# PEER experts of a decoder block: 32 of 256 tokens by fetched expert rows, 224 tokens dense, all up steps ahead of one down pass

## The chip, the cores and the metric

The kernel runs on one core of a Trainium2 chip. The metric is the device time of one execution in microseconds (us). Before the change it is 2338.79 us, the median of three executions (2336.44 to 2342.29). The engines that matter are TensorE (PE; PEld is its weight load, a row of its own), VectorE (DVE), ScalarE (ACT), GpSimd (POOL) and SyncE (SP), the last of which here only issues DMAs. Every engine takes its own instructions in a fixed order.

## The reference, cut to what matters

The block first mixes 256 tokens of width 2048 (sparse attention, a pooling branch, an output projection). The change leaves that part as it is. Then comes PEER: each token picks 8 x 16 = 128 of 16384 single-neuron experts by a product of two key lists, and sums what they give.

```python
def peer_channel_mixer(h, w_peer_q, peer_keys, peer_u, peer_v):
    ...                                   # sub: scores against 2 x 128 keys, 8 heads
    s_top, i_top = lax.top_k(sub, PEER_TOPK)                       # 16 of 128, twice
    cand = s_top[..., 0, :, None] + s_top[..., 1, None, :]
    cand_idx = i_top[..., 0, :, None] * PEER_KEYS + i_top[..., 1, None, :]
    ...
    best, pos = lax.top_k(cand, PEER_TOPK)                         # 16 of 256
    experts = jnp.take_along_axis(cand_idx, pos, axis=-1)
    gates = jax.nn.softmax(best, axis=-1)
    ...
        u = peer_u[ec]
        a = jax.nn.gelu(jnp.einsum('cd,ced->ce', hc, u), approximate=False)
        vv = peer_v[ec]
        return jnp.einsum('ce,ced->cd', (a * gc), vv)
```

`peer_u` and `peer_v` are 16384 rows of 2048 float32 each, 128 MB a table.

## The kernel before

All tokens go through all experts densely. A gate matrix, 16384 experts by 256 tokens and zero where a token did not pick the expert, keeps what counts. The experts come in 128 blocks of 128, the blocks in 4 chunks of `CH` = 32, and the stages follow each other in the order up 0, up 1, down 0, down 1, up 2, up 3, down 2, down 3.

To keep float32 accuracy each product is made of three matmuls (`mm3`, L129 to L133): a float32 operand is split into a rounded high part and the rest (`split`, L117 to L123). ACT casts the high part `wH` (L121), DVE subtracts it from the source to give `wL` (L122). There are three buffers each of `wH` and `wL`, half a block apiece, so the splitters can run one and a half blocks ahead of PE. Weights land in `raw`, four buffers of 1 MB (`RAW`), by DMAs that SP issues (L110 to L115).

`up` (L738 to L745) holds a block of `u` as weights, 128 x 128 at a time, and streams the 256 tokens past: 16 x 3 matmuls of 256 columns a block, then a Gelu on ACT (L744) into `r1` to `r4`. `down` (L762 to L797) holds activations as weights (`aH` L776, `aL` L777) and streams rows of `v` past, 512 columns a matmul: 24 matmuls for each block and half of the output, 48 in all.

Beside `up` runs side work in pieces: the routing (top 16 lists L581 to L584, decoding, softmax), 32 calls of `gates_build` (L697 to L725) that make the gate matrix from one-hot tiles on DVE (L707 to L710), PE (L718) and ACT (L721) and write it to device memory by 16 POOL DMAs, the last 16 rows of the modulation matrix (`ada`, L135 to L138, one DVE pass of 128 x 2048 each), and turning `x` token-first (L752). `step` hands out 1.25 pieces a block (`R_G`) and a modulation row every fourth block (`R_U`). `gates_apply` (L727 to L733) reads the gates back and multiplies. The source order is not the last word: the framework's scheduler interleaves the pieces and fixes the order on each engine when the program is built.

Of the kernel before, what the change touches and what calls it, by code (L numbers as in the profile page):

```python
# [39 lines left out]
def kernel(  # L40
# [647 lines left out]

    def new_a(c):
        if c % 2 == 0:  # L690
            return [px.tile([P, ND, T], F32, name=f"r{i}") for i in (2, 3)]
        return [main.tile([P, ND, T], F32, name="r1"), px.tile([P, ND, T], F32, name="r4")]

    gdram = dram.tile([P, 64, P, 4], F32, name="gdram")
    gstage = {}

    def gates_build(x):  # L697
        t1 = TB * x
        o2 = px.tile([P, TB // 2, P, 2], F16, name="o2", bufs=2)
        o1 = [px.tile([P, TB // 2, P, 2], F16, name=f"o1{q}", bufs=1 + q) for q in range(2)]  # L700

        def per_token(src):
            return (src[:, t1:t1 + TB].rearrange("p (g t) -> p g t", t=2)[:, :, None, :]
                    .to_broadcast([P, TB // 2, P, 2]))

        every = iota2[:, None].to_broadcast([P, TB // 2, P, 2])
        dve.tensor_tensor(o2, every, per_token(idxT[1]), ALU.is_equal)  # L707
        dve.tensor_tensor(o1[1], every, per_token(idxT[0]), ALU.is_equal)
        for q in range(2):
            dve.tensor_tensor(o1[q], o1[1], per_token(gT[q]), ALU.mult)  # L710
        if x % 2 == 0:
            gstage[0] = stream.tile([P, D], F32, name="raw", bufs=RAW)
        for y in range(2):
            ps = gps.tile([P, 512], F32, name="gp")
            for i in range(4):
                for q in range(2):
                    g, k = 2 * y + i // 2, i % 2
                    pe.matmul(ps[:, P * i:P * i + P], o2[:, g, :, k], o1[q][:, g, :, k],  # L718
                              start=q == 0, stop=q == 1)
            n = 2 * (x % 2) + y  # L720
            act.mul(gstage[0][:, 512 * n:512 * n + 512].rearrange("p (i t) -> p i t", t=4),  # L721
                    ps.rearrange("p (t i) -> p i t", i=P), 1.0 / GATE_SCALE)
        if x % 2 == 1:
            g = 2 * (x - 1)
            nc.gpsimd.dma_start(out=gdram[:, g:g + 4].rearrange("p g i t -> p (g i t)"), in_=gstage[0])  # L725

    def gates_apply(a, c, z):  # L727
        raw = stream.tile([P, D], F32, name="raw", bufs=RAW)
        raw = raw.rearrange("p (g i t) -> p g i t", g=16, t=4)
        nc.sync.dma_start(out=raw, in_=gdram[:, 16 * z:16 * z + 16, CH * c:CH * c + CH])  # L730
        for k in range(2):
            av = a[k][:, :, 64 * z:64 * z + 64].rearrange("p i (g t) -> p i g t", t=4)
            dve.tensor_tensor(av, av, raw[:, :, 16 * k:16 * k + 16].rearrange("p g i t -> p i g t"), ALU.mult)  # L733

    def g_pieces(a, c):
        return [lambda z=z: gates_apply(a, c, z) for z in range(4)]

    def up(c, a, per_unit):  # L738
        for e in range(CH):
            ps = accp.tile([P, 512], F32, name="acc")[:, :T]  # L740
            w = load_split(u_in[CH * c + e])
            for d in range(ND):
                mm3(ps, w[d // 8], (d % 8) * P, hH[:, d], hL[:, d], d == 0, d == ND - 1)
            act.activation(a[e // 16][:, e % 16], ps, AF.Gelu)  # L744
            per_unit(e)  # L745

    xtok = xT.rearrange("p j (t d) -> p j t d", t=2)

    def flip_x(q, t):
        ps = gps.tile([P, 512], F32, name="gp")  # L750
        for i in range(4):
            pe.transpose(ps[:, P * i:P * i + P], xtok[:, 4 * q + i, t], ident)  # L752
        act.copy(xtok[:, 4 * q:4 * q + 4, t], ps.rearrange("p (i d) -> p i d", d=P))
# [176 lines left out]
```

## Time and profile before

| what | value |
|---|---|
| median of three executions | 2338.79 us (2336.44 to 2342.29) |
| profiled execution, its own time | 2337.39 us |
| its span, first to last instruction | 2335.5 us |
| PE busy | 2248.0 us, 96% |
| DVE busy | 1577.1 us, 68% |
| ACT busy | 1043.2 us, 45% |
| mean of the DMAs | 226 GB/s |
| mean granted TensorE clock | 0.981 of full speed |

The profiled execution's own time is 1.9 us above its span. A stretch of the span is read by what each engine did in it: an engine that is busy all the time bounds the stretch, and an engine that idles there costs nothing. The time of one matmul is read from the starts of neighbouring ones, since matmuls overlap in the pipeline and each is longer than the distance to the next.

### The profile page before, as it was taken

How to read it: one execution, taken by the hardware profiler on the slowest of the kernel's cores; microseconds unless marked ns; L12 is line 12 of the kernel's file. 1: busy time of each engine (PE TensorE's matmuls, PEld its weight loads, DVE VectorE, ACT ScalarE, POOL GpSimd, SP SyncE). 2: the span in 40 equal slices, each digit the busy share in tenths (PEclk: the TensorE clock that was granted, in tenths of full speed). 3: DMA queues.
4: the chain of work that ended last, by engine and by line, in shares of the span. 5: the costliest groups of instructions: out<-in, count | busy, mean ns of one | idle time of the engine just before them, and what ended most of it. 6: DMA issues, size and time to landing. Idle time of an engine off the chain costs nothing.

```text
span 2335.5 us, 37425 instructions
## 1 busy us (share of the span) xinstructions
PE 2248.0 (96%) x15280; PEld 2061.2 (88%) x15280; DVE 1577.1 (68%) x2419; ACT 1043.2 (45%) x1555; POOL 12.9 (1%) x27
## 2 busy tenths in 40 slices
PE   6999999999989988998899999999999999999998
PEld 5899987999989988997898888889999999888887
DVE  7888877779687998586556656655445445566565
ACT  4543441844344443344444444444444444444443
POOL 0000000000000000000000000000000000000000
PEclk7999999999999999998999999999999999999999
DMA  8888865688755644655587555455457556655563
GB/s 332 334 316 305 299 239 216 247 296 311 283 219 214 227 167 181 245 210 209 219 268 243 184 192 194 184 191 188 181 181 246 192 186 210 232 192 185 189 208 109
DMA packets 126414, 527.02 MB, mean 226 GB/s; under 512 B 8425, under 2 KB 46337, under 8 KB 85793
## 3 DMA queue, kind: packets, MB, share of 16 engines
q1 hardware_dynamic: 123794, 507.68, 60.2%
q0 software_dynamic: 2448, 16.94, 1.8%
q8 instruction: 120, 1.97, 0.3%
q14 instruction: 52, 0.43, 0.0%
HBM read 505.71 MB, written 18.89 MB: 225 GB/s over the span
## 4 chain that ended last, share of the span: by engine, by line
PE 85%; DVE 9%; DMA 4%; issue 1%; ACT 1%; DVEq 0%; ACTq 0%
PE acc L133 16%; PE acc L131 16%; PE acc L132 16%; PE acc L784 10%; PE acc L783 10%; PE acc L785 10%; DMA raw<-in_ada_dram 2%; PE acc L504 2%; DVE wL L122 2%; DVE raw L137 2%; PE gp L718 1%; DVE o L710 1%; DMA raw<-in_wgrp_dram 1%; ACT wH L121 1%; PE mps L206 0%
## 5 line engine op out<-in xcount | busy, mean ns | idle before, releaser
L122 DVE TENSOR_TENSOR wL<-raw,wH 128x1024 fp32r<-128x1024 f32 (+2 forms) x738 | 873.1, 1187 | 589.6 <-ACT wH L121 588.6
L121 ACT CAST wH<-raw 128x1024 fp32r<-128x1024 f32 (+2 forms) x738 | 751.8, 1021 | 1020.5 <-PE acc L132 580.6
L131 PE MATMUL acc<-hH,wH 128*128 128x256 f32 x3248 | 931.1, 287 | 19.1 <-ACT wH L121 17.6
L133 PE MATMUL acc<-hH,wL 128*128 128x256 f32 x3248 | 926.5, 286 | 9.2 <-DVE wL L122 8.8
L132 PE MATMUL acc<-hL,wH 128*128 128x256 f32 x3248 | 925.8, 285 | 0.1
L131 PEld LDWEIGHTS acc<-hH,wH 128*128 128x128 f32 x3248 | 630.3, 194 | 23.9 <-ACT wH L121 21.1
L133 PEld LDWEIGHTS acc<-hH,wL 128*128 128x128 f32 x3248 | 628.9, 194 | 13.8 <-DVE wL L122 13.5
L132 PEld LDWEIGHTS acc<-hL,wH 128*128 128x128 f32 x3248 | 630.4, 194 | 0.8 <-DVE hL L568 0.3
L784 PE MATMUL acc<-wH,aL 128*128 128x512 f32 x1024 | 404.7, 395 | 0.2
L785 PE MATMUL acc<-wL,aH 128*128 128x512 f32 x1024 | 404.1, 395 | 0.0
L783 PE MATMUL acc<-wH,aH 128*128 128x512 f32 x1024 | 400.3, 395 | 0.0
L137 DVE CUSTOM_DVE_ANT_0 raw<-raw,cb 128x2048 f32<-128x2048 f32 x96 | 219.5, 2286 | 32.9 <-DMA raw<-in_ada_dram 32.6
L784 PEld LDWEIGHTS acc<-wH,aL 128*128 128x128 f32 x1024 | 193.0, 188 | 47.4 <-DVE aL L777 2.8
L783 PEld LDWEIGHTS acc<-wH,aH 128*128 128x128 f32 x1024 | 192.9, 188 | 45.0
L785 PEld LDWEIGHTS acc<-wL,aH 128*128 128x128 f32 x1024 | 192.9, 188 | 44.8
L777 DVE TENSOR_TENSOR aL<-r,aH 128x256 fp32r<-128x256 f32 x256 | 106.5, 417 | 0.0
L776 ACT CAST aH<-r 128x256 fp32r<-128x256 f32 x256 | 102.1, 400 | 6.5 <-PE acc L785 3.3
L744 ACT ACTIVATE r<-acc 128x256 f32<-128x256 f32 x128 | 48.6, 380 | 75.0 <-PE acc L133 75.0
L710 DVE TENSOR_TENSOR o<-o,gT 128x1024 f16<-128x1024 f16 x64 | 43.9, 686 | 49.2 <-PE gp L718 49.2
L718 PE MATMUL gp<-o,o 128*128 128x128 f16 x512 | 44.8, 237 | 32.1 <-DVE o L710 26.4
L132 PE MATMUL acc<-m,wH 128*128 128x256 f32 x256 | 72.1, 282 | 0.0
L718 PEld LDWEIGHTS <-o 128*128 128x128 f16 x512 | 34.3, 106 | 38.1 <-DVE o L710 20.0
(216 smaller groups left out, 1447.3 us busy)
## 6 DMA issues: line engine op xcount, KB each, us to landing
raw<-in_u_dram SPq DMA_DIRECT2D x128, 1024.0 KB, 4.8
raw<-in_v_dram SPq DMA_DIRECT2D x128, 1024.0 KB, 4.9
raw<-in_ada_dram SPq DMA_DIRECT2D x96, 1024.0 KB, 5.9
raw<-in_wgrp_dram SPq DMA_DIRECT2D x43, 768.0 KB, 6.3
raw<-in_ybr_dram SPq DMA_DIRECT2D x16, 1024.0 KB, 6.8
raw<-in_wga_dram SPq DMA_DIRECT2D x16, 1024.0 KB, 4.9
raw<-in_wout_dram SPq DMA_DIRECT2D x16, 1024.0 KB, 5.7
raw<-in_wpq_dram SPq DMA_DIRECT2D x16, 1024.0 KB, 5.9
```

The lines of the kernel that those rows point to most:

```text
L121: act.copy(wH[:, :n], src)
L122: dve.tensor_tensor(wL[:, :n], src, wH[:, :n], ALU.subtract)
L131: pe.matmul(ps, wH, xH, start=start, stop=False, **kw)
L132: pe.matmul(ps, wH, xL, start=False, stop=False, **kw)
L133: pe.matmul(ps, wL, xH, start=False, stop=stop, **kw)
L137: dve.tensor_tensor_reduce(raw, raw, cb, scale=1.0, scalar=0.0, op0=ALU.mult, op1=ALU.add, accum_out=modr[:, i:i + 1])
L718: pe.matmul(ps[:, P * i:P * i + P], o2[:, g, :, k], o1[q][:, g, :, k], start=q == 0, stop=q == 1)
L776: act.copy(aH, src)
L777: dve.tensor_tensor(aL, src, aH, ALU.subtract)
L783: pe.matmul(ps[t][k], tH, wH[:, vs], start=first, stop=False)
L784: pe.matmul(ps[t][k], tL, wH[:, vs], start=False, stop=False)
L785: pe.matmul(ps[t][k], tH, wL[:, vs], start=False, stop=final)
```

## The change

The first 32 tokens (`AS`) leave the dense path. For them the code fetches the expert rows by index: four copies of 32 tokens lie on 128 partitions (`SG` = 4), each partition has 32 of the 128 experts of its token, and 32 gathers of 128 rows of `u` and 32 of `v` (8 KB a row, 1 MB a gather, issued by POOL at L787) bring them into two buffers that share the old tile `r1`. DVE makes each dot product with the token (`sparse_up`, one 128 x 2048 pass a gather, L799) and each weighted sum (`sparse_down`, L813 and L815). Each DVE pass, once issued in the code, is followed by the fetch two further on, which takes the buffer that the pass frees. `tokens_h` lays the tokens out for it.

The other 224 tokens (`N`) stay dense. `up` runs over all 128 blocks at a stretch and stores its activations to device memory (`adram`) by an ACT DMA every four blocks. One down pass then holds `v` blocks as weights and streams 224 columns of `aH` or `aL` past: 128 blocks x 16 x 3 matmuls. Activations and gates come back eight blocks at a time into `ab` and `gb`, one buffer each (`gate_load`), are multiplied and split (`gate_split`: L839, L843, L844). The gates of the 224 tokens are 28 builds and 14 writes. At the end 16 matmuls add the sparse sums to the same accumulators, and the output is written feature-first. The turning of `x` and the spreading of the modulation (L752, L759) go. The remaining modulation rows stand between `sparse_up` and `sparse_down` in the list of side work, and `step` hands out 0.72 pieces a block in up and 0.56 in down.

On POOL the whole of the expert part was 16 writes of gates:

```order
L629 IOTA iota_8293 128x256
L725 DMA gdram<-raw 128x2048 x16
L925 UNCONDITIONAL_BRANCH
L925 ISA
```

Now the 64 gathers (`r_15011` is the tile with the two buffers, `idxS` the row numbers, `gS` the gates) stand there too:

```order
L632 IOTA iota_8293 128x256
L685 DMA idxS<-eU 32x32 x4
L787 DMA r_15011<-in_urow_dram,idxS 128x2048 x2
L704 DMA gS<-cand 32x32 x4
L787 DMA r_15011<-in_urow_dram,idxS 128x2048 x25
L761 DMA gdram<-raw 128x2048
L787 DMA r_15011<-in_urow_dram,idxS 128x2048 x5
L787 DMA r_15011<-in_v_dram,idxS 128x2048 x32
L761 DMA gdram<-raw 128x2048 x13
L981 UNCONDITIONAL_BRANCH
```

Thirteen of the 14 gate writes come behind the last gather in POOL's queue.

On DVE, in the up part before, splits (`wL`) stand evenly between the side work (here gate building, late in up 1):

```order
L710 TENSOR_TENSOR o_12231<-o_12232,gT_8291 128x1024
L122 TENSOR_TENSOR wL<-raw,wH 128x1024
L710 TENSOR_TENSOR o_12232<-o_12232,gT_8292 128x1024
L707 TENSOR_TENSOR o_12258<-iota_8293,idxT_8290 128x1024
L122 TENSOR_TENSOR wL<-raw,wH 128x1024
L708 TENSOR_TENSOR o_12260<-iota_8293,idxT_8289 128x1024
L141 TENSOR_TENSOR mod<-modr,vecs 128x16
L122 TENSOR_TENSOR wL<-raw,wH 128x1024 x2
```

Now, from up block 24 on, the sparse work stands there; at the end of the dot products and the start of the sums (`hs` is the running sum) it reads:

```order
L799 ISA r_15011,aS<-r_15011,hs 128x2048
L799 ISA aS 128x1
L807 TENSOR_TENSOR wS<-aS,gS 128x32
L813 TENSOR_SCALAR hs<-r_15011,wS 128x2048
L815 SCALAR_TENSOR_TENSOR hs<-r_15011,wS,hs 128x2048
L125 TENSOR_TENSOR wL<-raw,wH 128x1024
L815 SCALAR_TENSOR_TENSOR hs<-r_15011,wS,hs 128x2048 x2
L125 TENSOR_TENSOR wL<-raw,wH 128x1024
L815 SCALAR_TENSOR_TENSOR hs<-r_15011,wS,hs 128x2048 x3
L125 TENSOR_TENSOR wL<-raw,wH 128x1024
L815 SCALAR_TENSOR_TENSOR hs<-r_15011,wS,hs 128x2048 x2
L125 TENSOR_TENSOR wL<-raw,wH 128x1024
```

All 64 sparse passes stand within 25 splits, the 275th to the 299th of DVE's 738, of which the first 226 belong to the part ahead of the experts and two go to each block. So they lie between up blocks 24.5 and 37, two or three passes to a split.

On DVE in the down pass each split had its own small piece of activations before:

```order
L777 TENSOR_TENSOR aL<-r_8297,aH 128x256
L122 TENSOR_TENSOR wL<-raw,wH 128x1024
L777 TENSOR_TENSOR aL<-r_8297,aH 128x256
L122 TENSOR_TENSOR wL<-raw,wH 128x1024
L777 TENSOR_TENSOR aL<-r_8297,aH 128x256
```

Now four blocks of splits stand between the pieces, and the multiplication by the next eight blocks' gates stands right behind the last use of the old buffer:

```order
L839 TENSOR_TENSOR ab<-ab,gb 128x896 x2
L125 TENSOR_TENSOR wL<-raw,wH 128x1024 x8
L844 TENSOR_TENSOR aL<-ab,aH 128x896
L125 TENSOR_TENSOR wL<-raw,wH 128x1024 x8
L844 TENSOR_TENSOR aL<-ab,aH 128x896
L839 TENSOR_TENSOR ab<-ab,gb 128x896 x2
L125 TENSOR_TENSOR wL<-raw,wH 128x1024 x8
```

So between the piece that reads `ab` last and the first multiplication in the refilled `ab` no split is queued.

The diff, cut to its core (the functions taken out stand in the listing above):

```diff
-CH = 32
+AS = 32
+N = T - AS
+SG = P // AS
 RAW = 4
-R_K, R_Y, R_GA, R_WO, R_PQ, R_U = 0.6, 0.4, 0.7, 0.6, 0.3, 0.25
+R_K, R_Y, R_GA, R_WO, R_PQ = 0.6, 0.4, 0.7, 0.6, 0.3
 TB = 8
-R_G = 1.25
+R_UP, R_DN = 0.72, 0.56
...
+        if t == 0 and s == 0:
+            dve.tensor_scalar(eS, sel[0:AS], 128.0, None, op0=ALU.mult)
+        elif t == 0:
+            dve.tensor_tensor(eS, eS, sel[0:AS], ALU.add)
+            dve.tensor_copy(eU, eS)
+            for g in range(SG):
+                nc.gpsimd.dma_start(out=idxS[AS * g:AS * g + AS], in_=eU[:, AS * g:AS * g + AS])
...
+        if t == 0:
+            ef = e.rearrange("p a b -> p (a b)")
+            for g in range(SG):
+                nc.gpsimd.dma_start(out=gS[AS * g:AS * g + AS], in_=ef[0:AS, AS * g:AS * g + AS])
...
+    gdram = dram.tile([P, N // 16, P, 16], F32, name="gdram")
+    adram = dram.tile([P, P, N], F32, name="adram")
+    made = {}
...
+    def gates_sum(x):
+        o2, o1 = made.pop(x)
+        half = x % 2
+        if half == 0:
+            made["stage"] = stream.tile([P, D], F32, name="raw", bufs=RAW)
+        stage = made["stage"].rearrange("p (i t) -> p i t", t=16)
+        for y in range(2):
+            ps = gps.tile([P, 512], F32, name="gp")
+            for i in range(4):
+                for q in range(2):
+                    g, k = 2 * y + i // 2, i % 2
+                    pe.matmul(ps[:, P * i:P * i + P], o2[:, g, :, k], o1[q][:, g, :, k],
+                              start=q == 0, stop=q == 1)
+            t0 = 8 * half + 4 * y
+            act.mul(stage[:, :, t0:t0 + 4], ps.rearrange("p (t i) -> p i t", i=P), 1.0 / GATE_SCALE)
+        if half == 1:
+            nc.gpsimd.dma_start(out=gdram[:, (x - AS // TB) // 2].rearrange("p i t -> p (i t)"), in_=made["stage"])
+
+    def gates_build(x):
+        if x < T // TB:
+            gates_hot(x)
+        if x > AS // TB:
+            gates_sum(x - 1)
+
...
+    def gathered(n, table):
+        if "gat" not in made:
+            made["gat"] = main.tile([P, ND, T], F32, name="r1").rearrange("p (b a) t -> p b (a t)", b=2)
+        rows = made["gat"][:, n % 2]
+        nc.gpsimd.indirect_dma_start(out=rows, out_offset=None, in_=table,
+                                     in_offset=bass.IndirectOffsetOnAxis(ap=idxS[:, n:n + 1], axis=0))
+        return rows
...
+    def fetch(n, table):
+        made["rows", n % 2] = gathered(n, table)
+
+    def sparse_up(n):
+        rows = made["rows", n % 2]
+        dve.tensor_tensor_reduce(rows, rows, made["h"], scale=1.0, scalar=0.0, op0=ALU.mult, op1=ALU.add,
+                                 accum_out=aS[:, n:n + 1])
+        if n + 2 < AS:
+            fetch(n + 2, urows)
+        else:
+            fetch(n + 2 - AS, vrows)
+        if n == AS - 1:
+            act.activation(aS, aS, AF.Gelu)
+            dve.tensor_tensor(wS, aS, gS, ALU.mult)
+
+    def sparse_down(n):
+        rows = made["rows", n % 2]
+        if n == 0:
+            made["o"] = px.tile([P, D], F32, name="hs")
+            dve.tensor_scalar(made["o"], rows, wS[:, 0:1], None, op0=ALU.mult)
+        else:
+            dve.scalar_tensor_tensor(made["o"], rows, wS[:, n:n + 1], made["o"], op0=ALU.mult, op1=ALU.add)
+        if n + 2 < AS:
+            fetch(n + 2, vrows)
+
+    def up(e):
+        if e % 4 == 0:
+            made["a"] = px.tile([P, 4, N], F32, name="ast", bufs=3)
+        ps = accp.tile([P, 512], F32, name="acc")[:, :N]
+        w = load_split(u_in[e])
+        for d in range(ND):
+            mm3(ps, w[d // 8], (d % 8) * P, hH[:, d, AS:], hL[:, d, AS:], d == 0, d == ND - 1)
+        act.activation(made["a"][:, e % 4], ps, AF.Gelu)
+        if e % 4 == 3:
+            act.dma_start(out=adram[:, e - 3:e + 1], in_=made["a"])
+
+    def gate_load(b):
+        made["ab"] = px.tile([P, 8, N], F32, name="ab")
+        nc.sync.dma_start(out=made["ab"], in_=adram[:, 8 * b:8 * b + 8])
+        made["gb"] = px.tile([P, N // 16, 8, 16], F32, name="gb")
+        nc.sync.dma_start(out=made["gb"], in_=gdram[:, :, 8 * b:8 * b + 8])
+
+    def gate_split(h):
+        i = 4 * (h % 2)
+        av = made["ab"][:, i:i + 4].rearrange("p i (g t) -> p i g t", t=16)
+        dve.tensor_tensor(av, av, made["gb"][:, :, i:i + 4].rearrange("p g i t -> p i g t"), ALU.mult)
+        src = made["ab"][:, i:i + 4]
+        aH = px.tile([P, 4, N], F32R, name="aH", bufs=2)
+        aL = px.tile([P, 4, N], F32R, name="aL", bufs=2)
+        act.copy(aH, src)
+        dve.tensor_tensor(aL, src, aH, ALU.subtract)
+        made["act", h] = (aH, aL)
...
+    later = routing(1)
+    build = [lambda x=x: gates_build(x) for x in range(AS // TB, T // TB + 1)]
+    side += routing(0) + [lambda q=q: tokens_h(q) for q in range(4)]
+    for x in range(12):
+        side += [later.pop(0), build[x]]
+    side += later + build[12:]
+    side.append(lambda: (fetch(0, urows), fetch(1, urows)))
+    side += [lambda n=n: sparse_up(n) for n in range(AS)]
+    side += bg + [lambda: add_bias(GT2, 16)]
+    side += [lambda n=n: sparse_down(n) for n in range(AS)]
+
+    for e in range(P):
+        up(e)
+        step(R_UP)
+        if e == P - 12:
+            gate_load(0)
+        if e == P - 2:
+            gate_split(0)
+
+    po = [(accp.tile([P, 512], F32, name="acc") if q < 6 else gps.tile([P, 512], F32, name="gp"))
+          .rearrange("p (a t) -> p a t", a=2) for q in range(8)]
+
+    def products(e, w, j):
+        aH, aL = made["act", e // 4]
+        mm3(po[j // 2][:, j % 2, AS:], w, (j % 8) * P, aH[:, e % 4], aL[:, e % 4],
+            e == 0 and j % 2 == 0, e == P - 1, skip_group_check=True)
+
+    def finish_block(j):
+        x = xT[:, j]
+        dve.scalar_tensor_tensor(x, po[j // 2][:, j % 2], mod[:, GT2 + j:GT2 + j + 1], x, op0=ALU.mult, op1=ALU.add)
+        if j % 2 == 1:
+            nc.sync.dma_start(out=out[:, j - 1:j + 1, :], in_=xT[:, j - 1:j + 1, :])
+
+    for e in range(P - 2):
+        w = load_split(v_in[e])
+        for j in range(ND):
+            products(e, w[j // 8], j)
+        step(R_DN)
+        if e % 4 == 1 and e + 3 < P:
+            gate_split(e // 4 + 1)
+        if e % 8 == 2 and e + 6 < P:
...
     run_side(len(side))
+    for j in range(ND):
+        pe.matmul(po[j // 2][:, j % 2, 0:AS], made["o"][:, P * j:P * j + P], selS, start=False, stop=True,
+                  skip_group_check=True)
+    raws = [load(v_in[e]) for e in (P - 2, P - 1)]
+    for f in range(2):
+        ws = [split(raws[i][:, 1024 * f:1024 * f + 1024]) for i in range(2)]
+        for j in range(8 * f, 8 * f + 8):
+            for i in range(2):
+                products(P - 2 + i, ws[i], j)
+            finish_block(j)
```

## Rows read from the trace of the kernel before

**Rows 1.** The page: busy time of each engine, and the chain that ended last.
```profile
PE 2248.0 (96%) x15280; PEld 2061.2 (88%) x15280; DVE 1577.1 (68%) x2419; ACT 1043.2 (45%) x1555; POOL 12.9 (1%) x27
PE 85%; DVE 9%; DMA 4%; issue 1%; ACT 1%; DVEq 0%; ACTq 0%
```

**Rows 2.** Busy time by stage; the first column is the stretch in us.
```profile
core 0: us, PE busy (x) PEld busy (x) DVE busy (x) ACT busy (x) POOL busy (x), PEclk, DMA share, GB/s
0.00:774.00 774.00, 734.35 (x5497) 695.02 (x5498) 616.78 (x1087) 346.69 (x573) 4.35 (x11) 0.97 0.76 278
774.00:870.00 96.00, 86.38 (x709) 84.55 (x709) 94.43 (x239) 40.85 (x55) 1.10 (x2) 0.95 0.46 174
...
1243.00:1601.00 358.00, 357.90 (x1543) 289.47 (x1542) 217.08 (x283) 172.58 (x254) 0.00 (x0) 1.00 0.55 198
1601.00:1970.00 369.00, 369.00 (x3074) 368.87 (x3073) 172.73 (x149) 153.00 (x194) 0.00 (x0) 1.00 0.55 194
1970.00:2327.00 357.00, 356.90 (x1536) 288.53 (x1535) 218.05 (x284) 170.77 (x252) 0.00 (x0) 1.00 0.54 192
2327.00:2336.00 9.00, 1.27 (x6) 0.70 (x4) 4.20 (x7) 0.00 (x0) 0.00 (x0) 0.80 0.41 117
```

**Rows 3.** Busy time of up 0 and up 1 together, same columns.
```profile
774.00:1243.00 469.00, 428.58 (x3634) 418.62 (x3634) 348.25 (x614) 200.15 (x282) 8.54 (x16) 0.95 0.58 213
```

**Rows 4.** Timeline of PE in up 0: start, duration, line, operation, operands.
```profile
804.43 0.28 PE L132 MATMUL acc<-hL,wH 128*128 128x256 f32 x1
...
805.03 0.28 PE L131 MATMUL acc<-hH,wH 128*128 128x256 f32 x1
```

**Rows 5.** Timeline of PE in down 1.
```profile
1589.32 0.39 PE L784 MATMUL acc<-wH,aL 128*128 128x512 f32 x1
...
1590.95 0.39 PE L785 MATMUL acc<-wL,aH 128*128 128x512 f32 x1
```

**Rows 6.** Timeline of PEld, two weight loads behind a stall.
```profile
1243.68 0.19 PEld L783 LDWEIGHTS acc<-wH,aH 128*128 128x128 f32 x1
1243.79 0.19 PEld L784 LDWEIGHTS acc<-wH,aL 128*128 128x128 f32 x1
```

**Rows 7.** Timeline of PE, plain float32 matmuls of 256 and of 128 columns.
```profile
400.15 2.21 PE L504 MATMUL acc<-m,raw 128*128 128x256 f32 x9
...
1239.96 1.27 PE L759 MATMUL gp<-ident,mod 128*128 128x128 f32 x10
```

**Rows 8.** Groups by line and shape: count, busy us, mean ns, idle before.
```profile
L122 DVE TENSOR_TENSOR wL<-raw,wH 128x1024 fp32r<-128x1024 f32 x645 | 786.3, 1222 | 579.8 <-ACT wH L121 579.2
...
L137 DVE CUSTOM_DVE_ANT_0 raw<-raw,cb 128x2048 f32<-128x2048 f32 x96 | 219.5, 2286 | 32.9 <-DMA raw<-in_ada_dram 32.6
...
L710 DVE TENSOR_TENSOR o<-o,gT 128x1024 f16<-128x1024 f16 x64 | 43.9, 686 | 49.2 <-PE gp L718 49.2
...
L581 DVE MAX8 stop<-r 128x8 f32<-128x128 f32 x64 | 17.8, 283 | 0.5
...
L582 DVE FIND_INDEX8 pos<-best,cand 128x8 uint32<-128x256 f32 x32 | 13.4, 418 | 0.0
...
L725 POOL DMA_DIRECT2D gdram<-raw x16 | 8.5, 534 | 378.3 <-ACT raw L721 378.3
...
L137 DVE DVE_READ_ACCUMULATOR2_ANT modr<- 128x1 f32 x96 | 7.8, 82 | 0.0
...
L752 PE MATMUL gp<-ident,xT 128*128 128x128 f32 x32 | 4.7, 281 | 0.7 <-ACT xT L753 0.4 <-ACT raw L721 0.3
...
L466 DVE SCALAR_TENSOR_TENSOR pT<-ws,pl 128x512 f32<-128x512 f32 x4 | 2.7, 686 | 5.8 <-PE mps L480 5.7
```

**Rows 9.** DMA issues: count, KB each, median us from issue to landing.
```profile
raw<-in_v_dram SPq DMA_DIRECT2D x128, 1024.0 KB, 4.9
...
gdram<-raw POOLq DMA_DIRECT2D x16, 1024.0 KB, 4.5
raw<-gdram SPq DMA_DIRECT2D x16, 1024.0 KB, 5.7
...
raw<-fd SPq DMA_DIRECT2D x1, 1024.0 KB, 8.1
```

**Rows 10.** Busy time of a stretch near the start, columns as in Rows 2.
```profile
20.00:36.00 16.00, 2.60 (x6) 1.02 (x6) 15.93 (x34) 2.10 (x6) 0.52 (x1) 0.55 0.95 362
```

More of the change, by code (lines that the diff above doesn't have):

```diff
@@ L60 @@
     v_in: bass.AP,
+    urow_in: bass.AP,
     out: bass.AP,
@@ L687, in gates_flip @@
         dve.scalar_tensor_tensor(gT[1][:, sl], ps, GATE_SCALE, gT[0][:, sl], op0=ALU.mult, op1=ALU.subtract)
[L689 to L753, printed above, removed]
@@ new lines, in gates_sum @@
+    def gates_sum(x):
[7 more added lines that the diff above has]
+            for i in range(4):
+                for q in range(2):
+                    g, k = 2 * y + i // 2, i % 2
[5 more added lines that the diff above has]
+            nc.gpsimd.dma_start(out=gdram[:, (x - AS // TB) // 2].rearrange("p i t -> p (i t)"), in_=made["stage"])
@@ new lines, in gates_build, with tokens_h @@
+    def gates_build(x):
[3 more added lines that the diff above has]
+            gates_sum(x - 1)
+    def tokens_h(q):
+        if q == 0:
+            made["h"] = px.tile([P, D], F32, name="hs")
+        ps = gps.tile([P, 512], F32, name="gp")
+        reps = []
+        for src in (hH, hL):
+            rep = px.tile([P, 4, SG, AS], F32R, name="o2", bufs=2)
+            act.copy(rep, src[:, 4 * q:4 * q + 4, None, 0:AS].to_broadcast([P, 4, SG, AS]))
+            reps.append(rep.rearrange("p a g i -> p a (g i)"))
+        for i in range(4):
+            for n in range(2):
+                pe.matmul(ps[:, P * i:P * i + P], reps[n][:, i], identR, start=n == 0, stop=n == 1)
+        act.copy(made["h"][:, 512 * q:512 * q + 512], ps)
@@ L819, with step @@
     owed = [0.0]
-    def step(e):
-        owed[0] += R_G
+    def step(rate):
+        owed[0] += rate
         run_side(int(owed[0]))
         owed[0] -= int(owed[0])
-        pace(R_U)
-    a0 = new_a(0)
-    up(0, a0, step)
-    a1 = new_a(1)
-    side += g_pieces(a0, 0)
-    up(1, a1, step)
-    while bg:
-        pace(1.0)
-    add_bias(GT2, 16)
-    run_side(len(side))
-    for q in range(4):
-        spread_gate(q)
-    side += g_pieces(a1, 1)
-    down(0, a0, step, False)
-    run_side(len(side))
@@ L908, in _arrays @@
         "v": f["peer_v"][0].reshape(P, P, D),
+        "urow": f["peer_u"][0],
     }
@@ L928 @@
     o = np.asarray(r.results[0]["out_0_dram"])
-    return o.reshape(1, T, D)
+    return np.ascontiguousarray(o.transpose(2, 1, 0)).reshape(1, T, D)
```

87 lines of the change are left out of this document (26 added, 61 removed).

## The prediction, made before the change was run

> **What bounds the kernel now.** I read the page's shares and chain first, then busy time by stage, then single matmuls. PE is busy 96% of the span and owns 85% of the chain that ended last [rows 1]. By stage the picture sharpens: from 1243 to 2327 us PE is busy 1083.8 of 1084 us, while DVE is busy 217, 173 and 218 us in stretches of about 360 [rows 2]. There only PE's own work counts. In up 0 and up 1 PE is idle 469 - 428.6 = 40 us [rows 3], 10 of them in the first 96 us, where DVE is busy 94.4 of 96 with the routing [rows 2]. So the kernel is bound by PE, with one place where DVE already equals it. A change pays if PE gets less work and DVE still keeps ahead of PE everywhere. DVE can only be 1.5 blocks ahead (three half buffers of wL), about 8 us of PE work, so it is the local order on DVE that matters, and not its total.
>
> **Dense matmuls, the gain.** Up: 6144 matmuls of 256 columns, six starts in 0.60 us, 0.120 us each [rows 4]. Down: 3072 of 512 columns, seven in 1.63 us, 0.233 each [rows 5]. Together 737 + 715 = 1452 us. After: 12288 matmuls of 224 columns, each with weights of its own. No such matmul is in the trace. From below, scaling rows 4 by columns gives 0.105; from above, nothing is saved against 256 columns, 0.120. Two weight loads behind a stall start 0.11 apart [rows 6], and plain float32 matmuls of 128 columns, ten in 1.27 with a last of 0.28, are 0.11 apart [rows 7]. A new weight every 128 x 128 needs that long, so I take 0.111: 682 + 682 = 1364 us, **-88**. The turning of x and the modulation's spreading, 64 matmuls of about 0.11 [rows 7, 8], go: **-6**, less the 16 merge matmuls of 0.11, which leaves it near -5; I keep -6, the difference is below what I can read.
>
> The Trainium skill, "TensorE: Matmul & The Clock Gate", section "Back-to-back issue gap", gives an isolated gap of N/2.4 + 2.5 ns for N columns, so 95.8 ns here, and says that it under-counts at small N. By it the dense work would be 1177 us, a gain of 275. The trace disagrees already at 256 columns (109 by the rule, 120 measured).
>
> **The sparse work, the loss.** 64 DVE passes of 128 x 2048 float32 are added, and 64 gathers of 1 MB. A pass costs 2.29 us with the product and sum of L137, plus 0.08 for the reading of the sum [rows 8]; a scalar_tensor_tensor of 512 columns takes 0.69 [rows 8], so four times that is no cheaper. By the built order all 64 stand among 25 splits, up blocks 24.5 to 37. PE needs only 12.5 x 48 x 0.111 = 66 us for these blocks. DVE needs 64 x 2.3 = 147, plus 25 splits of about 1.14 (1.22 less overlap) = 28, plus 14 gate passes of 0.6 = 8 [rows 8]: 184 us. That alone costs PE 184 - 66 - 8 = **110 us**, even if every gather landed at once. This is the lower bound.
>
> They don't land at once. A fetch reuses the buffer that its pass frees, so a buffer's cycle is pass 2.37 + POOL's issue 0.53 [rows 8] + landing. For the landing of 1 MB the rows give 4.5 (POOL's queue, writing), 4.9, 5.7 (reading device memory in pieces) and 8.1 us [rows 9]; I take 5.7, as the gather reads scattered rows and shares the engines with the u stream. Cycle 8.6, two buffers, 4.3 us a gather, 64 x 4.3 = 275 us, and PE loses 275 - 66 - 8 = **+201**. With 8.1 it is 11.0 / 2 x 64 = 352, **+278**. The fastest that the engines show is 362 GB/s [rows 10], 2.9 us for 1.05 MB, 185 us for all, so bandwidth doesn't lower the floor. The splits queued behind a waiting pass wait with it, and PE behind them. PE's clock will drop there, as it stood at 0.55 where PE was busy 2.6 of 16 us [rows 10]; at its lower level the 66 us become 133, still under 275, so this is hidden.
>
> The Trainium skill, "DMA: Bandwidth & Descriptors", section "Measured", gives 6.15 us for a 1 MB load issued by GpSimd. By it the stretch would be 290 us and the sum 15 more; the trace's POOL writes of that size land in 4.5.
>
> **Routing.** On DVE 162 instructions of the top lists and the decoding now stand among the first nine u splits. At 0.28 to 0.42 us for a search, and one index load of 0.08 with every second [rows 8], that is about 60 us against 4 to 4.5 blocks of PE, 24 us; a smaller bunch follows 15 blocks later. Before, these were spread over twice the blocks and cost 10 us there [rows 2]. I take 36 + 14 - 10 = **+40** (0 if they were spread as before; 75 if the 8 us ahead are not there at the start).
>
> **Gate building.** 28 builds replace 32, and their PE part comes a step later, which can return up to the other 30 us of up 0 and up 1 [rows 3]. But 13 of 14 gate writes wait behind the gathers on POOL, with the stage, one of four raw buffers, held until then. I take **+30** (-30 to +60).
>
> **The down pass.** ab and gb have one buffer each. SP's load waits until DVE and ACT have read the old half, then 1.8 MB land, and the multiplication is queued ahead of the next splits. From rows 9 that is 5 to 8.1 us in which DVE stands, 15 times. PE has at most 8 us in hand, less the passes and casts after the landing, so I take 3.5 us each, **+52** (0 to 15 x 8.1 = 120). Beside the waits DVE has room: 16 splits of 1.14 and four passes of about 1.1 are 23 us against 42 of PE for eight blocks. The 16 remaining modulation rows, 16 MB and 16 passes of 2.37 us, fall in some 20 blocks here; 36 MB plus gates and activations in 107 us is near 362 GB/s, and they take raw buffers from v: **+45** (0 to 70). Behind the last matmul, 8.3 us of DVE and output remain now [rows 2]; one block and its 256 KB write do much the same after: 0.
>
> **Sum.** -88 - 6 + 201 + 40 + 30 + 52 + 45 = +274, on the profiled execution's 2337.4: 2611 us. That execution is 1.4 us under the median, so **2612 us** forecast. All low ends together give -14, all high ends (with 0.111) +509.
>
> **Rivals.**
> 1. *Faster: PE streams by columns.* At 0.105 the dense work is 1290 us, -162, and if the sparse stretch costs only DVE's own time (110, 4 more for the shorter PE work) and the other four terms vanish, the time is 2337 - 168 + 114 = 2283. It decides where routing, gates, gb waits and modulation together stay below 54 us. For it speaks DVE's 50% idle share in long stretches; against it rows 6, and that each term has a place in the order. By the skill's gap rule above the same case would be about 2180. Chance 0.05, with no change 0.02 between.
> 2. *No gain per matmul.* At 0.120 the dense work is 1475, so +23 in place of -88: 2612 + 111 - 7 (longer PE cover in the sparse stretch) = 2716. For it: every weight load in the 256-column stages is paced so; against: rows 6. Chance 0.13.
> 3. *The reduced float32 format falls to the plain rate below 256 columns.* Plain float32 runs 256 columns in (2.21 - 0.38) / 8 = 0.229 us [rows 7], so 224 in 0.20. 12288 x 0.089 = 1094 more, of which some 250 of the waits would hide: about 3450. Nothing in the trace has fewer than 256 columns in this format. Chance 0.08.
> 4. *Gathers much slower than plain transfers.* Each 2 us more of landing is 64 us more. At 12 us: 14.9 / 2 x 64 = 477, 2814 in all. Chance 0.09.
>
> **Chances.** The forecast, 2470 to 2760, holds 0.63, rival 2 0.13, rival 4 0.09, rival 3 0.08, rival 1 and no change 0.07. The range 2440 to 2820 takes in the forecast, rival 2 and rival 4, and leaves out 0.08 above, 0.07 below and some edges. A difference under 0.3% (7 us) can't be told from none. Faster 0.05, same 0.02, slower 0.93.
>
> **What would show it.** In the profile after: matmuls of 224 columns 0.111 us apart; one stretch of some 275 us in up where PE is busy about a quarter, DVE waits for the gathers at L799 and L815, and the chain of waits runs through them; gathers landing in 5 to 6 us; about 15 waits of DVE at L839 for ab or gb, several us each; a short bunch of searches at up's beginning. I am wrong if PE stays above 90% busy through up, or if the gathers land so late that the stretch passes 400 us.

## The result, and the profile after

The changed kernel takes 2696.93 us (median, 2692.28 to 2698.83) against 2340.54 for the kernel before in the same session: a ratio of 1.152, 95% interval 1.149 to 1.155. That is 356 us more, where 274 were forecast. The time lies inside the range. Three terms were too small, those of the sparse stretch, the gate waits and the modulation rows, and the reason given for the last was wrong.

First the pace of the new matmuls. Timeline of PE in the up pass of the changed kernel (start us, duration us, line, operation, operands), answering to [rows 4]:

```profile
1449.80 0.27 PE L136 MATMUL acc<-hH,wL 128*128 128x224 f32 x1
...
1451.14 0.28 PE L136 MATMUL acc<-hH,wL 128*128 128x224 f32 x1
```

Twelve starts in 1.34 us, 0.112 us each, the value taken. So a block of 48 matmuls needs about 5.33 us of PE. The next view counts the matmuls of line L136, the third of every three, by stage of the changed kernel; the count divided by 16 is the number of blocks done. Columns: stretch, its length, busy time and count of PE and PEld for that line alone, granted clock, DMA share, GB/s.

```profile
774.00:900.00 126.00, 78.89 (x265) 56.34 (x265) 0.85 0.49 170
900.00:966.00 66.00, 30.81 (x97) 22.40 (x97) 0.79 0.34 123
966.00:1266.00 300.00, 79.47 (x201) 59.40 (x201) 0.64 0.72 265
1266.00:1650.00 384.00, 255.82 (x904) 180.58 (x904) 0.93 0.60 213
1650.00:1851.00 201.00, 156.64 (x563) 110.27 (x563) 0.96 0.64 219
1851.00:2100.00 249.00, 147.08 (x487) 105.25 (x486) 0.86 0.58 205
2100.00:2682.00 582.00, 435.34 (x1550) 307.12 (x1550) 0.96 0.59 204
```

The up pass ends at 1851 us. Stage by stage, time less blocks x 5.33: routing (774 to 966) 192 - 22.6 blocks = 71 us lost; the sparse stretch (966 to 1266) 300 - 12.6 blocks = 233; the rest of up 585 - 91.7 blocks = 96, in which PE also does the gate building; down 831 - 127.3 blocks = 152, of which 86 before 2100 us, where the modulation rows are. For comparison, up 0 and up 1 before took 469 us for 64 blocks of 48 x 0.120 = 5.76, so 100 us beyond the dense work [rows 3, 4], and both down stretches lost next to nothing [rows 2].

In the sparse stretch DVE reads like this (changed kernel, timeline of DVE; behind a row in brackets the idle time before it and what ended it):

```profile
999.23 2.29 DVE L799 CUSTOM_DVE_ANT_0 r<-r,hs 128x2048 f32<-128x2048 f32 x1 [1.86 <-DMA r<-in_urow_dram,idxS]
1001.45 0.08 DVE L799 DVE_READ_ACCUMULATOR2_ANT aS<- 128x1 f32 x1
1004.80 2.29 DVE L799 CUSTOM_DVE_ANT_0 r<-r,hs 128x2048 f32<-128x2048 f32 x1 [3.27 <-DMA r<-in_urow_dram,idxS]
1007.02 0.08 DVE L799 DVE_READ_ACCUMULATOR2_ANT aS<- 128x1 f32 x1
1007.02 1.22 DVE L125 TENSOR_TENSOR wL<-raw,wH 128x1024 fp32r<-128x1024 f32 x1
1008.16 2.28 DVE L799 CUSTOM_DVE_ANT_0 r<-r,hs 128x2048 f32<-128x2048 f32 x1
...
1013.67 2.29 DVE L799 CUSTOM_DVE_ANT_0 r<-r,hs 128x2048 f32<-128x2048 f32 x1 [3.22 <-DMA r<-in_urow_dram,idxS]
...
1018.34 1.22 DVE L125 TENSOR_TENSOR wL<-raw,wH 128x1024 fp32r<-128x1024 f32 x1
```

One split (L125) every 11 us, where PE needs one every 2.7. Between them DVE works on sparse passes or stands for a gather; the splits are queued behind, though their weights have landed (SP itself stands up to 43 us there for a split to free a raw buffer). The waits of DVE in this stretch, and the groups and DMAs of the sparse work (busy us and mean ns; median us to landing):

```profile
DVE hs L815 <- DMA r<-in_v_dram,idxS: 60.4, 24, 5.2
DVE r L799 <- DMA r<-in_urow_dram,idxS: 57.2, 23, 5.9
```
```profile
L799 DVE CUSTOM_DVE_ANT_0 r<-r,hs 128x2048 f32<-128x2048 f32 x32 | 73.2, 2290 | 57.2 <-DMA r<-in_urow_dram,idxS 57.2
L815 DVE SCALAR_TENSOR_TENSOR hs<-r,wS,hs 128x2048 f32<-128x2048 f32 x31 | 72.9, 2351 | 60.7 <-DMA r<-in_v_dram,idxS 60.4
...
L787 POOL DMA_INDIRECT r<-in_v_dram,idxS x32 | 43.6, 1364 | 109.5 <-DVE hs L815 80.7 <-DMA r<-in_v_dram,idxS 16.7 <-DVE aS L799 7.5
L787 POOL DMA_INDIRECT r<-in_urow_dram,idxS x32 | 43.0, 1345 | 174.4 <-DVE aS L799 168.1 <-ACT wH L124 5.1 <-issue 1.2
```
```profile
r<-in_urow_dram,idxS POOLq DMA_INDIRECT x32, 6.5
r<-in_v_dram,idxS POOLq DMA_INDIRECT x32, 6.1
```

The dot products cost what [rows 8] said, 2.29 us, and the weighted sums 2.35. The waits for gathers, 60.4 + 57.2, make 118 of the 300 us. The issue takes 1.35 us on POOL and not 0.53. The landing is counted from the start of the issue, here and in [rows 9], so it holds the issue: the gather issued at 1007.37 lands 6.3 us later, just before the pass of 1013.67. Its mean over the 64 gathers is 6.9 us, where the prediction took 0.53 + 5.7 = 6.2 for issue and landing together. A buffer's cycle is then 2.37 + 6.9 = 9.3, halved 4.6, against 300 / 64 = 4.7 seen.

In the down pass, here around 1900 us, DVE and SP's queue of the changed kernel read:

```profile
1895.18 1.08 DVE L844 TENSOR_TENSOR aL<-ab,aH 128x896 fp32r<-128x896 f32 x1
1900.69 2.09 DVE L839 TENSOR_TENSOR ab<-ab,gb 128x896 f32<-128x896 f32 x2 [4.43 <-DMA ab<-adram]
1902.70 1.22 DVE L125 TENSOR_TENSOR wL<-raw,wH 128x1024 fp32r<-128x1024 f32 x1
1911.81 2.29 DVE L140 CUSTOM_DVE_ANT_0 raw<-raw,cb 128x2048 f32<-128x2048 f32 x1 [7.90 <-DMA raw<-in_ada_dram]
...
1921.25 1.23 DVE L125 TENSOR_TENSOR wL<-raw,wH 128x1024 fp32r<-128x1024 f32 x1 [3.73 <-ACT wH L124]
1927.52 2.29 DVE L140 CUSTOM_DVE_ANT_0 raw<-raw,cb 128x2048 f32<-128x2048 f32 x1 [5.04 <-DMA raw<-in_ada_dram]
```
```profile
1896.29 0.33 SPq L832 DMA_DIRECT2D ab<-adram  x1
1902.81 0.52 SPq L834 DMA_DIRECT2D gb<-gdram  x1
1903.94 0.41 SPq L117 DMA_DIRECT2D raw<-in_ada_dram  x1
...
1922.50 0.33 SPq L117 DMA_DIRECT2D raw<-in_ada_dram  x1
```

DVE stands 4.4 us for ab, whose load goes out as L844 ends. The modulation rows do the same. SP waits until a split frees a raw buffer, and on DVE the row's pass stands right behind that split: the split of 1902.70 ends at 1903.92, the row's load goes out at 1903.94 and DVE stands 7.9 us for it; the split of 1921.25 ends at 1922.48, the load goes out at 1922.50 and DVE stands 5.0. All 12 rows of this stretch go so, each load within 0.04 us of the end of the split ahead of its pass, and DVE stands 72.5 us for them. This is a wait that the prediction did not name.

### The profile page after: what moved, and what is told of

It is laid out like the page before. It is cut to its first block, busy times and chain, and to the rows that moved or that the text cites. A ratio compares the mean times of both kernels' runs of the same rounds, so it can differ in the third digit from the quotient of the medians.

```text
span 2694.0 us, 43015 instructions
## 1 busy us (share of the span) xinstructions
PE 2302.6 (85%) x18288; PEld 2245.4 (83%) x18288; DVE 1631.1 (61%) x2232; ACT 982.6 (36%) x1325; POOL 102.7 (4%) x97
## 5 line engine op out<-in xcount | busy, mean ns | idle before, releaser
L125 DVE TENSOR_TENSOR wL<-raw,wH 128x1024 fp32r<-128x1024 f32 (+2 forms) x738 | 870.3, 1189 | 621.1 <-ACT wH L124 619.7
L136 PE MATMUL acc<-hH,wL 128*128 128x224 f32 (+1 forms) x3248 | 948.3, 293 | 207.7 <-DVE wL L125 207.5
L134 PE MATMUL acc<-hH,wH 128*128 128x224 f32 (+1 forms) x3248 | 949.0, 293 | 28.5 <-ACT wH L124 27.0
L135 PE MATMUL acc<-hL,wH 128*128 128x224 f32 (+1 forms) x3248 | 941.6, 290 | 0.1
L136 PEld LDWEIGHTS acc<-hH,wL 128*128 128x128 f32 x3248 | 664.3, 205 | 218.0 <-DVE wL L125 217.7
L136 PE MATMUL acc<-aH,wL 128*128 128x224 f32 x1536 | 440.3, 287 | 87.1 <-DVE wL L125 87.1
L134 PE MATMUL acc<-aH,wH 128*128 128x224 f32 x1536 | 438.6, 286 | 1.1 <-DVE xT L883 0.7
L135 PE MATMUL acc<-aL,wH 128*128 128x224 f32 x1536 | 437.4, 285 | 0.0
L136 PEld LDWEIGHTS acc<-aH,wL 128*128 128x128 f32 x1536 | 311.4, 203 | 92.1 <-DVE wL L125 92.1
L134 PEld LDWEIGHTS acc<-aH,wH 128*128 128x128 f32 x1536 | 311.3, 203 | 3.0 <-DVE xT L883 2.6
L135 PEld LDWEIGHTS acc<-aL,wH 128*128 128x128 f32 x1536 | 311.4, 203 | 0.0
L134 PE MATMUL gp<-aH,wH 128*128 128x224 f32 x512 | 147.4, 288 | 0.7 <-DVE xT L883 0.7
L136 PE MATMUL gp<-aH,wL 128*128 128x224 f32 x512 | 146.8, 287 | 0.0
L815 DVE SCALAR_TENSOR_TENSOR hs<-r,wS,hs 128x2048 f32<-128x2048 f32 x31 | 72.9, 2351 | 60.7 <-DMA r<-in_v_dram,idxS 60.4
L799 DVE CUSTOM_DVE_ANT_0 r<-r,hs 128x2048 f32<-128x2048 f32 x32 | 73.2, 2290 | 57.2 <-DMA r<-in_urow_dram,idxS 57.2
```

The lines of the kernel that those rows point to most:

```text
L125: dve.tensor_tensor(wL[:, :n], src, wH[:, :n], ALU.subtract)
L134: pe.matmul(ps, wH, xH, start=start, stop=False, **kw)
L135: pe.matmul(ps, wH, xL, start=False, stop=False, **kw)
L136: pe.matmul(ps, wL, xH, start=False, stop=stop, **kw)
L799: dve.tensor_tensor_reduce(rows, rows, made["h"], scale=1.0, scalar=0.0, op0=ALU.mult, op1=ALU.add, accum_out=aS[:, n:n + 1])
L815: dve.scalar_tensor_tensor(made["o"], rows, wS[:, n:n + 1], made["o"], op0=ALU.mult, op1=ALU.add)
```

## The experiments

All edits are to the changed kernel. `cut[0]` is DVE's latest split; `tc.issue_after(x)` only queues what the block issues on x's engine behind x, it waits for nothing.

**Sparse passes where the source calls for them.**

```diff
+    def behind(f, *a):
+        with tc.issue_after(cut[0].ins):
+            f(*a)
-    side += [lambda n=n: sparse_up(n) for n in range(AS)]
+    side += [lambda n=n: behind(sparse_up, n) for n in range(AS)]
```
(and the same for `sparse_down`)

> Only DVE's order is changed: each of the 64 sparse passes is queued behind the split of the block at which the source calls for it (up block 94 to down block 91, one in one to two blocks) instead of 64 passes among 25 splits. All work stays. In the changed kernel the sparse stretch takes 300 us for 12.6 up blocks that need 67 us of PE, a loss of 233. Theory (the local order on DVE makes that loss): 2697 - 233, and a few us for passes that delay a split, so 2465 to 2500. Rival (the gathers and passes cost the same wherever they stand, by traffic, by POOL's queue or by the two buffers): 2640 to 2700.

2501.0 us (ratio to before 1.071, 1.067 to 1.075). One us above the expected range. Of the 233 us, 196 went by an order alone. The rival falls, as the gathers, the passes and the two buffers are the same.

**All side work in place.**

```diff
-        run_side(int(owed[0]))
+        behind(run_side, int(owed[0]))
```

> As the run before, but all side work (routing, gate building, modulation rows, sparse passes) is queued on DVE behind the split of the block at which the source calls for it. Routing then costs little: the changed kernel lost 192 - 22.6 x 5.33 = 71 us between 774 and 966. Theory (bunches of any side work cost PE what exceeds DVE's lead of 8 us): 50 to 90 less than the run with only the sparse passes in place, so 2380 to 2440. Rival (routing costs its chain of dependent steps, and a later routing makes the gates late): the same as that run within 15 us, or slower.

2389.5 us (1.022, 1.019 to 1.024), another 112 less, more than the 50 to 90 expected, though the time lies in the range. Where the gates are built, 966 to 1700 us, no more blocks are done than in the run before. Ten more are done by 966 us, 53 us of PE, and 8.6 more from 1700 to 1900 us, 46 us: the modulation rows are spread too, and DVE, which stood 75.2 us for them in the run before, stands for none.

**Only the gate products of the down pass in place.**

```diff
-            gate_split(e // 4 + 1)
+            behind(gate_split, e // 4 + 1)
```

> Only DVE's order in the down pass is changed: the multiplication by the gates of the next half (L839) and its split (L844) are queued behind the split three blocks ahead of their use, so the loads of ab and gb have about 16 us to land before DVE asks for them. From 2100 to 2682 us the changed kernel lost 582 - 96.9 x 5.33 = 65 us. Theory (DVE waits for the loads with splits queued behind, 3 us of PE wait and as much again by the lower clock after it, some 14 times): 2620 to 2645. Rival (the loads themselves take raw buffers, DMA time or SP's queue from the v stream): 2680 to 2700.

2613.9 us (1.118, 1.115 to 1.120), 83 less, a little more than expected. Busy time by stage (columns as in [rows 2]) shows that PE is never idle where only gate products were at stake, with the same loads and the same single buffers (from 2100 us; the modulation rows end ahead of it):

```profile
2100.00:2300.00 200.00, 200.00 (x1794) 200.00 (x1793) 108.85 (x93) 86.33 (x84) 0.00 (x0) 1.00 0.70 235
2300.00:2390.00 90.00, 90.00 (x809) 90.00 (x808) 50.28 (x44) 39.31 (x39) 0.00 (x0) 1.00 0.70 237
```

**No sparse work at all.**

```diff
-    side.append(lambda: (fetch(0, urows), fetch(1, urows)))
-    side += [lambda n=n: sparse_up(n) for n in range(AS)]
+    side.append(lambda: made.update(o=made['h']))
-    side += [lambda n=n: sparse_down(n) for n in range(AS)]
```

> Gathers and sparse passes are left out, so the 32 sparse tokens get a meaningless sum; everything else stays, and the 16 modulation rows move from the down pass to the end of up by themselves. Theory: the sparse stretch's loss of 233 goes, and of the 86 us lost around the modulation rows in the down pass 30 to 70: 2395 to 2440. If the run with the sparse passes in place comes within 70 us above this one, sparse work costs next to nothing where it has room. Rival (the loss is in gate building and in the down pass, and the sparse stretch only hides it): 2550 or more.

2445.9 us (1.045, 1.042 to 1.049), 251 less than the changed kernel and 55 less than with the passes in place; the forecast was a little too low. DVE still stands 65.5 us for the modulation rows and 51.7 for ab. Without the sparse work the dense part alone is still slower than the kernel before, so the bunch of sparse passes is not the only fault.

**Both in place** (the second and third edit).

> All side work and the gate products of the down pass are queued on DVE where the source calls for them (the second and third run together). If the two losses are separate the gains add: 2390 - 83 = 2307, with 2295 to 2330 as the range. Rival (both come from one shortage, of DMA or of raw buffers, so that the second change only moves the wait): 2345 to 2390. Below 2332 it is faster than the kernel before.

2290.0 us (0.979, 0.975 to 0.983): 2.1% faster than the kernel before, and 17 us below what the two gains together would give. Busy time by stage of this run:

```profile
966.00:1266.00 300.00, 274.85 (x2424) 270.34 (x2422) 190.50 (x326) 126.99 (x177) 8.13 (x11) 0.95 0.58 207
1266.00:1400.00 134.00, 117.11 (x966) 114.34 (x966) 72.04 (x77) 50.37 (x70) 5.80 (x7) 0.89 0.61 216
1400.00:1500.00 100.00, 99.75 (x893) 99.57 (x892) 73.47 (x64) 43.40 (x55) 23.21 (x14) 1.00 0.96 356
1500.00:1600.00 100.00, 99.52 (x891) 99.34 (x890) 72.73 (x63) 43.37 (x54) 19.97 (x12) 1.00 0.97 366
```

From 1400 to 1600 us the DMAs carry 356 to 366 GB/s, gathers and u together, and PE is busy 99.6%. What is left is lost while gates are built, 966 to 1400 us.

**Passes without gathers.**

```diff
-        if n + 2 < AS:
-            fetch(n + 2, urows)
-        else:
-            fetch(n + 2 - AS, vrows)
```
(also in `sparse_down`; the dot product is scaled by 0.001)

> The changed kernel, with 4 gathers instead of 64: all 64 DVE passes stay and read old rows again (scaled down, so the sums are meaningless for the 32 tokens). They stand in 8.5 up blocks. Theory (DVE's own time is about half of the stretch, the landing of the gathers the other half): 64 x 2.3 + 17 x 1.14 + 8 = 174 us against 8.5 x 5.33 = 45 of PE, a loss of 121 to 129 in place of 233, so 2575 to 2605. Rival (the landing alone sets the stretch and DVE's passes fit beside it): 2460 to 2500. Rival (DVE alone sets it): 2670 or more.

2581.3 us (1.104, 1.101 to 1.108), inside the theory's bounds (in this order the passes stand in 8.5 blocks, not 12.5, and the trace has two gathers, not four). DVE now works without a gap and still delivers one split in some 10 us:

```profile
1006.01 1.23 DVE L125 TENSOR_TENSOR wL<-raw,wH 128x1024 fp32r<-128x1024 f32 x1
1007.15 2.30 DVE L799 CUSTOM_DVE_ANT_0 r<-r,hs 128x2048 f32<-128x2048 f32 x1
...
1016.00 1.24 DVE L125 TENSOR_TENSOR wL<-raw,wH 128x1024 fp32r<-128x1024 f32 x1
```

So 116 of the 233 us are the waits for landing and issue, as the 118 us of DVE's waits above say, and the other 117 DVE's own passes, close to the prediction's lower bound of 110.

**Modulation rows early, beside both in place, and alone.**

```diff
-    side += bg + [lambda: add_bias(GT2, 16)]
+    side.append(lambda: add_bias(GT2, 16))
...
         step(R_UP)
+        behind(pace, R_U)
```
(`R_U` is 0.25, a row every fourth block)

> As the run with both in place, and the 12 modulation rows that remain are loaded and summed in the first 48 up blocks, one in four blocks, instead of within 20 blocks of the down pass. Theory (in the down pass their loads, the v blocks, ab and gb and a gather ask for more than the 362 GB/s that the profile of before showed, and DVE waits for them with splits queued behind): 50 to 75 less than that run, 2235 to 2270. Rival (12 MB and 12 passes cost the same beside routing and gate building): no change within 15.

> The changed kernel with only the 12 modulation rows moved to the first 48 up blocks; the sparse passes and the gate products stay bunched. In the changed kernel the stretch 1851 to 2100 us lost 86, of which four gate waits of some 5.5 are 22. Theory: that loss of about 60 goes, some 5 of the rows now stand in the sparse stretch and add 2.4 each there: 2640 to 2665. Rival (the loss there is the gate waits and the start of the down pass): 2685 to 2710.

Alone 2632.1 us (1.125, 1.121 to 1.130), 65 less, a little more than expected: the loss around the rows is real. But beside both in place 2295.8 (0.980, 0.975 to 0.984), no change: the first of these expectations missed. The rows cost nothing there, although the DMAs carry 349 GB/s where they stand in the run with both in place (1640 to 1746 us), against 205 in the changed kernel (1851 to 2100 us, above). So bandwidth was not the cause.

Nor were ab and gb. With only the gate products in place DVE stands for ab no more and still stands 58.9 us for the 12 rows; 57 us are lost there (1851 to 2100 us), 36 of them PE standing. With only the side work in place DVE stands for none of the rows, though it stands 83.4 us for ab. The cause is the row's place on DVE, right behind the split that frees its buffer.

**A stage of its own for the gates, then late eviction too.**

```diff
-            made["stage"] = stream.tile([P, D], F32, name="raw", bufs=RAW)
+            made["stage"] = px.tile([P, D], F32, name="gst")
-            made["a"] = px.tile([P, 4, N], F32, name="ast", bufs=3)
+            made["a"] = px.tile([P, 4, N], F32, name="ast", bufs=2)
```

> As the run with the side work and the gate products in place, and the gate stage gets a buffer of its own (the activation stage gives one of its three), so all four raw buffers serve the weights. In that run the stretch 966 to 1400 us, where the gates are built, still loses PE 42 us of idle time and a granted clock of 0.89 to 0.95, and SP waits 95 us there for gate writes to free a raw buffer. Theory (the held raw buffer makes u late): 20 to 40 less, 2250 to 2270. Rival (ACT's order makes it: the eviction of the gate sums stands ahead of the casts, and ACT waits in it for PE): no change within 10.

2224.6 us (0.951, 0.949 to 0.954), 65 less than with both in place, about twice what was expected. In that run SP waited so in 1000 to 1400 us (us in all, times, longest):

```profile
SPq L117 <- DMA gdram<-raw: 94.7, 7, 18.7
```

With a stage of its own the same stage of the profile is:

```profile
966.00:1266.00 300.00, 297.95 (x2807) 297.30 (x2807) 219.58 (x345) 144.60 (x204) 9.20 (x13) 0.99 0.69 244
1266.00:1400.00 134.00, 129.02 (x1159) 128.29 (x1158) 89.83 (x82) 58.83 (x78) 19.60 (x13) 0.97 0.84 309
```

The second edit moves the eviction behind the next block's casts on ACT:

```diff
+    def gates_out():
+        ...
+        with tc.issue_after(cut[1].ins):       # ACT's latest cast
+            for o, i in outs:
+                act.mul(o, i, 1.0 / GATE_SCALE)
```

> As the run before, and the eviction of the gate sums is traced one block later and queued on ACT behind the casts of the next block. If ACT's order makes the loss of the gate stretch, 30 to 60 less than the run with the side work and the gate products in place: 2230 to 2260, 3 to 5% below the kernel before. If the held raw buffer made it, the same as the run before within 10.

2218.5 us (0.948, 0.946 to 0.950), within 10 of the run before. The held raw buffer made the loss, not ACT's order. This is the fastest version that computes the whole block: 5.2% below the kernel before.

**Fewer columns.**

```diff
-            mm3(ps, w[d // 8], (d % 8) * P, hH[:, d, AS:], hL[:, d, AS:], d == 0, d == ND - 1)
+            mm3(ps[:, :192], w[d // 8], (d % 8) * P, hH[:, d, AS:AS + 192], hL[:, d, AS:AS + 192], ...)
```

> The run before (own stage, late eviction) with 192 columns instead of 224 in the 6144 matmuls of the up pass, so 32 tokens get the activations of others; weights, loads and splits stay. Theory (a new weight of 128 x 128 every matmul sets the pace, 0.111 us): the matmuls stay 0.111 apart and the time within 10 of 2219. Rival (columns set the pace): 192 / 224 x 0.111 = 0.095 apart, 6144 x 0.016 = 97 us less, 2120 to 2140, unless DVE or the loads then bound it.

2220.2 us, as with 224 columns (0.951, 0.948 to 0.953). Timeline of PE:

```profile
1449.77 0.28 PE L136 MATMUL acc<-hH,wH 128*128 128x192 f32 x1
...
1451.00 0.27 PE L138 MATMUL acc<-hH,wL 128*128 128x192 f32 x1
```

Eleven starts in 1.23 us, 0.112: the columns don't set the pace at 192 or 224.

**In place, without sparse work.** The edit of the fourth run on top of the fastest version.

> The run with own stage and late eviction, without gathers and sparse passes, so the 32 sparse tokens get a meaningless sum. It measures what the sparse work costs where it stands one pass in one to two blocks, behind PE. Theory (hidden there): 2205 to 2219, a cost of at most 14 of the 233 us that the same work cost in a bunch. Rival (traffic at 340 to 355 GB/s in 1400 to 2000 us delays u and v): 2180 or less.

2212.3 us (0.946, 0.943 to 0.949): the sparse work costs 6 us where it has room, within the scatter of either run, against 233 in a bunch.

## Why the prediction was right, and where its sizes were off

- *Dense work, -88.* Right: 0.112 against 0.111 taken, so 12288 matmuls give back 80 to 88. (The -6 beside it is 7.0 - 1.8 = 5.3 by its own rows, a difference too small to read.) The reason given, that a new weight sets the pace, fits the run with 192 columns, which shows that the columns don't. Nor is it a fixed cost of every matmul: in the changed kernel 16 gate matmuls of 128 columns, each with new f16 weights of 128 x 128 (L756, from 1473.88 us), take 1.08 us, about 0.055 apart. That it is the load of the float32 weight fits both and was not tried apart. The Trainium skill, "TensorE: Matmul & The Clock Gate", section "LDWEIGHTS", gives columns / 1.2, 107 ns for 128; the trace agrees within 5% for the float32 weights. The Trainium skill's gap rule that the prediction weighed (same page, section "Back-to-back issue gap") gives 95.8 ns at 224 columns and 82.5 at 192; neither is seen.
- *The sparse stretch, +201.* The right mechanism and place; measured 233. The term was mis-sized by the cycle: issue and landing together take 6.9 us and not 6.2, and the stretch 300 us and not 275. The other 7 us are the splits' lead of 8, which the prediction took off and the 233 leaves in, less 1 for the blocks (67 for 66). Placing the passes took 196 off, leaving out their gathers 116. The Trainium skill's 6.15 us for 1 MB, "DMA: Bandwidth & Descriptors", section "Measured", is a span without the issue; the trace has about 5.5 for that, 6.9 less 1.35.
- *Routing +40 and gate building +30.* Together 71 + 96 = 167 us beyond the dense work in up, against 100 before: +67, where +64 were forecast with the -6 for the turning of x. That the raw buffer held by the stage costs up's loads was right: a stage of its own gave 65 us, once the order no longer hid it. The reason given, that the gate writes wait behind the gathers, was not. Of SP's waits for a gate write one, 41.6 us, lies in the gathers' stretch; eleven, 109.8 us, come behind it, where POOL stands idle until ACT has filled the stage. The buffer is held while two builds fill it.
- *Gate waits +52 and modulation rows +45.* Measured 152 in place of 97; this is most of the miss. From 2100 to 2682 us, 11 multiplications cost 65, 5.9 each and not 3.5. PE stands no longer than forecast there, 2.5 us a time (30.5 us in 12 waits for a split); the rest is matmuls at the lower clock after each wait (below), which the term left out. The modulation term failed in its reason: "36 MB plus gates and activations in 107 us is near 362 GB/s" is refuted, since 366 GB/s runs beside a PE that is 99.5% busy and the rows' stretch here had 205. It was 12 rows (not 16, four had gone earlier) whose passes stand on DVE right behind the split that lets their load start. That its 45 is of the order of the 65 that moving the rows gave is luck.
- *The rivals.* "PE streams by columns" and "no gain per matmul" fall by the 0.112; the plain float32 rate below 256 columns too; gathers do land later than the u and v loads (4.9 us in [rows 9]), but by 1.2 to 1.6 us in the median and not by 7.
- Sum of the misses: 32 (sparse) + 3 (up) + 55 (down) + 3 (12 us behind the last full block for 8.5 before) = 93, less some 9 us by which the losses above are too large, since 254.2 of the 256 blocks' matmuls are in the trace. That is 84, and 274 + 84 = 358, the difference of the two spans (2694.0 and 2335.5).
- *The signs.* The pace, one long stretch in up, and DVE's waits at L799, L815 and L839 came as named. PE is busy 124 of the 300 us, 41% and not a quarter, at a granted clock of 0.64, and the gathers land in 6.1 to 6.5 us in the median and not in 5 to 6.

## What to carry to other kernels

A change that moves work to an engine with a third of its time idle (DVE was busy 68%) can lose by the order alone: look at the built order for how much of the new work stands between two steps that feed the bound engine, and compare it with the buffers' lead, here 8 us. When the step that lets a transfer start and the step that uses it stand next to each other in an engine's queue, everything behind them pays the landing; three blocks of distance cost nothing and took 83 us away. Also count what a long-held buffer takes from the stream that shares its pool.

## What the runs showed of the hardware

A short wait of PE is paid twice. In the changed kernel's down pass PE stands 2.6 us for a split, its matmuls start 0.11 us apart at first, and then it runs at half the clock. Timeline of PE around 2261 us:

```profile
2258.56 0.27 PE L135 MATMUL acc<-aL,wH 128*128 128x224 f32 x1
2261.41 0.37 PE L136 MATMUL acc<-aH,wL 128*128 128x224 f32 x1 [2.58 <-DVE wL L125]
...
2262.42 0.42 PE L134 MATMUL acc<-aH,wH 128*128 128x224 f32 x1
2262.64 0.42 PE L135 MATMUL acc<-aL,wH 128*128 128x224 f32 x1
...
2265.20 0.41 PE L135 MATMUL gp<-aL,wH 128*128 128x224 f32 x1
2265.41 0.34 PE L136 MATMUL gp<-aH,wL 128*128 128x224 f32 x1
2265.60 0.27 PE L134 MATMUL acc<-aH,wH 128*128 128x224 f32 x1
```

From 2262.42 to 2265.41 the starts are 0.21 us apart, the 1.2 GHz level (granted clock 0.51): 14 intervals that cost 1.4 us more than at 2.4 GHz. From 2100 to 2682 us PE is idle 31.5 of the 65 us lost, so the slower matmuls cost about as much as the waits. In the sparse stretch the mean granted clock is 0.64. Gathers by index of 128 rows of 8 KB take 0.94 to 3.05 us of POOL to issue in the changed kernel, 1.35 on the mean. Their median landing grows from 6.1 and 6.5 us to 8.6 (v) and 9.4 (u) in the run with both in place, where the DMAs carry 336 to 366 GB/s (1400 to 2000 us); PE is busy 99% there all the same.
